# First transposes on two engines, a five-step key choice and an earlier-fed tail in a hard-max attention kernel

## The chip, the cores and the metric

The kernel runs on one core of a Trainium2 chip. The time is device microseconds (us) of one execution. An execution profile gives a span, about 1.8 us shorter than the time. A ratio is the mean time of one kernel's fast runs over the mean of the kernel before in the same rounds, with a 95% interval; it is therefore not quite the ratio of the medians that stand beside it.

The engines are PE (matmul), ACT (scalar engine), DVE (vector engine), POOL (it issues every gather here) and SP (it issues the stores). "PEclk" is the granted PE clock, as a share of full speed.

## The reference

```python
B, Sq, Sk, D = 4, 4096, 4096, 128        # q, k, v: float32
logits = np.matmul(q, k.transpose(0, 2, 1))
best = np.argmax(logits, axis=-1)        # one key for each query
return v[b_idx, best, :]                 # the value row of that key
```

## The kernel before

Queries are taken in 128 tiles of 128. For each tile, PE and ACT screen the keys in fp16, in groups of four keys; DVE folds the result into packed scores with the group's index in the low bits (`W`) and takes the eight best (`TOP`, a MAX8). For the best group the kernel then

1. computes the group's index on DVE (`cand`),
2. gathers that group's key differences with POOL (`kg`, one indirect gather per tile),
3. forms the dot products on DVE (`prod`, `p`, `p`, `D`, two tiles at a time: a "pair"),
4. picks the key within the group with a few small DVE operations, for a "piece" of eight or four tiles (`mx` ... `win`),
5. gathers the value rows with POOL (`vr`, one per tile) and stores them through SP.

Rows whose winner is uncertain are flagged and computed again in fp32. For the second half of the rows this happens at the very end: gathers `FR`, `FQ`, three `FK`, some DVE work, `FV`, then a branch on a count loaded from memory (`all_rows`, for rows too hard for this; not taken with these inputs), then one scatter of the repaired rows.

The parts that the change touches (`...` marks cuts):

```python
    for h in range(2):
        load_k(0, h, 0, 16)
    load_q(0, 0, 8)
    load_q(0, 8, NQT)
    ...
    def trn_half(b, u, h):            # transposes of k on PE; ACT alone copies them out
        ...
        if h == 1:
            nc.scalar.activation(out=kT[b % 2][:, u * 1024:(u + 1) * 1024], in_=ps, func=AF.Copy)

    def dots(c, x, m):
        ...
        yield "until", lambda: ("kg", x) in done, 2      # two tiles after the gather's place
        ...                                              # prod, p, p, D

    def pick(c, t0, t1):                                 # seven operations per piece
        ...
        nc.vector.tensor_reduce(out=mx[:, :, 0], in_=d, axis=AX_X, op=OP.max)
        nc.vector.scalar_tensor_tensor(out=near, in0=d, scalar=NEAR, in1=mx..., op0=OP.add, op1=OP.is_ge)
        nc.vector.tensor_reduce(out=CNT[:, t0:t1], in_=near, axis=AX_X, op=OP.add)
        nc.vector.tensor_tensor(out=lt, in0=d, in1=mx..., op=OP.is_lt)
        nc.vector.scalar_tensor_tensor(out=sel, in0=lt, scalar=float(1 << 20), in1=iotab[b]..., op0=OP.mult, op1=OP.add)
        nc.vector.tensor_reduce(out=wi, in_=sel, axis=AX_X, op=OP.min)
        nc.vector.scalar_tensor_tensor(out=win, in0=cand, scalar=4.0, in1=wi, op0=OP.mult, op1=OP.add)
        for j in range(n):
            late_q.append(lambda j=j: nc.gpsimd.indirect_dma_start(out=vr[:, j, :], out_offset=None, in_=v_flat,
                                                                   in_offset=IOA(ap=win[:, j:j + 1], axis=0)))
    ...
    def issue(it):                    # POOL's gathers of one tile: at most one key gather, then value gathers
        ...
        while near_q and (n < 1 or near_q[0] in marks):
            ...
        take_late(2 if n == 0 and len(late_q) > 4 or it >= T - 8 and it % 2 else 1)
    ...
    cuts = list(range(0, T - 16 + 1, 8)) + [T - x for x in (12, 8, 4, 0)]   # the pieces
    ...
    for it in range(T):               # the order of the instructions in one tile
        ...
        screen(it); fold(it - 1)
        step(it)                      # one operation of each running dots/pick
        top(it - 2)                   # MAX8
        gathers(it - 3)               # cand, and the key gathers into POOL's list
        step(it)
        issue(it)
    ...
    def flags_last(...):              # after the last MAX8
        ...
        late(LATE)                    # LATE = 8 value gathers first
        get(FR, rec, rr, P * T)
        get(FQ, q_flat, row, P * T)
        late(1)
        ...
        for r in range(3):
            get(FK[:, r, :], k4, gb[:, r:r + 1], B * NG)
        ...
        late(3)
        win = whole(exact(FK, FQ, gb, 3, "fe"))
        get(FV, v_flat, win, B * Sk)
        late(1 << 20)                 # all value gathers that are left
        ...
        all_rows()                    # the branch
        nc.gpsimd.indirect_dma_start(out=out_flat, out_offset=IOA(ap=rowk, axis=0), in_=FV, ...)
```

Of the kernel before, what the change touches and what calls it, by code (L numbers as in the profile page):

```python
# [7 lines left out]
FP32 = mybir.dt.float32  # L8
# [19 lines left out]
def kernel(ctx, tc, q, k, v, out):  # L28
# [6 lines left out]
    NG = Sk // 4  # L35

    k4 = k.rearrange("b (g f) d -> (b g) (f d)", f=4)
# [16 lines left out]
    k16 = [dr.tile([NG, 384], FP16, name=f"k16_{b}") for b in range(B)]  # L54
# [13 lines left out]
    def put_k(b, h):  # L68
        if b >= B:
            return  # L70
        src = natk[b % 2][:, h].rearrange("p (g f) d -> p g f d", f=4)
        nc.vector.tensor_tensor(out=kd[:, h], in0=src[:, :, 1:4, :], in1=src[:, :, 0:1, :].to_broadcast([P, 4, 3, P]),
                                op=OP.subtract)
        kb16 = k16[b].rearrange("(h p n) d -> p h (n d)", p=P, n=4)
        nc.sync.dma_start(out=kb16[:, h], in_=kd[:, h].rearrange("p g f d -> p (g f d)"))
# [9 lines left out]
    for h in range(2):  # L85
        load_k(0, h, 0, 16)
    load_q(0, 0, 8)
    load_q(0, 8, NQT)
# [3 lines left out]
    for i in range(2):  # L92
        ps = pp.tile([P, 1024], FP32, tag="u", name=f"warm_{i}")
        for j in range(8):
            nc.tensor.matmul(out=ps[:, (j % 2) * 512:(j % 2 + 1) * 512], lhsT=wz[:, 0:P], rhs=wz, start=True, stop=True)

    ident = cp.tile([P, P], FP32, tag="ident")
    masks.make_identity(nc, ident)
    identh = cp.tile([P, P], FP16, tag="identh")
# [3 lines left out]
    for h in range(2):  # L103
        put_k(0, h)
    D_t = [cp.tile([P, 8, 4], FP32, name=f"D{i}", tag=f"D{i}") for i in range(3)]
# [4 lines left out]
    for W in W_t:  # L110
        nc.gpsimd.iota(out=W.bitcast(U16)[:, 0::2].rearrange("p (h m r) -> p h m r", h=2, m=4),
                       pattern=[[-NG // 2, 2], [-1, 4], [-4, P]], base=NG - 1, channel_multiplier=0)

# [6 lines left out]
    iotab = [iota(f"iotab{b}", 4, b * Sk) for b in range(B)]  # L120
    iota4 = iotab[0]
# [4 lines left out]
    nc.vector.tensor_copy(out=iota_h, in_=iota_r)  # L126
# [17 lines left out]
    def trn_half(b, u, h):  # L144
        x = 2 * (u // 2)
        if h == 0:
            tk_t[u] = pp.tile([P, 1024], FP32, tag="u", name=f"tk_{b}_{u}")
        ps = tk_t[u]
        for m in range(4):
            o = ps[:, h * 512 + m * P:h * 512 + (m + 1) * P]  # L150
            nc.tensor.matmul(out=o, lhsT=natk[b % 2][:, h, 4 * m + x, :], rhs=identh, start=True, stop=False)
            nc.tensor.matmul(out=o, lhsT=natk[b % 2][:, h, 4 * m + x + 1, :],
                             rhs=identn if u % 2 else identh, start=False, stop=True)
        if h == 1:
            nc.scalar.activation(out=kT[b % 2][:, u * 1024:(u + 1) * 1024], in_=ps, func=AF.Copy)
# [17 lines left out]
    def trn_q(b, g):  # L173
        if b >= B:
            return
        ps = pp.tile([P, 1024], FP32, tag="u", name=f"tq_{b}_{g}")
        for i in range(8):
            nc.tensor.matmul(out=ps[:, i * P:(i + 1) * P], lhsT=natq[b % 2][:, g * 8 + i, :], rhs=identh,
                             start=True, stop=True)
        nc.scalar.activation(out=qT[b % 2][:, g * 1024:(g + 1) * 1024], in_=ps, func=AF.Copy)  # L180
# [54 lines left out]
    def gather(c, t0, n):  # L235
        c0, c1 = chunks[c]
        if t0 == c0:
            cand_t[c] = sp.tile([P, c1 - c0], U32, tag=f"cand{c1 - c0}", name=f"cand_{c}", bufs=3)
        x = cand_t[c][:, t0 - c0:t0 - c0 + n]
        nc.vector.tensor_scalar(out=x, in0=TOP.bitcast(U32)[:, t0:t0 + n, 0], scalar1=NG - 1, scalar2=NG - 1,  # L240
                                op0=OP.bitwise_and, op1=OP.bitwise_xor)
        kg = rp.tile([P, n, 3, P], FP16, tag=f"kg{n}", name=f"kg_{t0}", bufs=8)
        assert len(kg_t) < 8
        kg_t[t0] = kg
        for j in range(n):
            near_q.append(lambda j=j: nc.gpsimd.indirect_dma_start(  # L246
                out=kg[:, j].rearrange("p f d -> p (f d)"), out_offset=None, in_=k16[t0 // NQT],
                in_offset=IOA(ap=x[:, j:j + 1], axis=0)))
        mark = lambda: done.add(("kg", t0))
        marks.add(mark)  # L250
        near_q.append(mark)
        start(dots(c, t0, n), "dots", c)

    def dots(c, x, m):
        c0 = chunks[c][0]
        d = D_t[c % 3]
        b = x // NQT
        yield "until", lambda: ("kg", x) in done, 2
# [14 lines left out]
    def pick(c, t0, t1):  # L273
        n = t1 - t0
        b, qt = t0 // NQT, t0 % NQT
        d = D_t[c % 3][:, 0:n, :]
# [9 lines left out]
        nc.vector.tensor_reduce(out=CNT[:, t0:t1], in_=near, axis=AX_X, op=OP.add)  # L286
        done.add(("cnt", c))
        yield "cnt",
        lt = sp.tile([P, n, 4], FP32, tag=f"lt{n}", name=f"lt_{c}")
        nc.vector.tensor_tensor(out=lt, in0=d, in1=mx.to_broadcast([P, n, 4]), op=OP.is_lt)  # L290
        yield "dve",
        sel = sp.tile([P, n, 4], FP32, tag=f"sel{n}", name=f"sel_{c}")
        nc.vector.scalar_tensor_tensor(out=sel, in0=lt, scalar=float(1 << 20),
                                       in1=iotab[b].unsqueeze(1).to_broadcast([P, n, 4]), op0=OP.mult, op1=OP.add)
        yield "dve",
        wi = sp.tile([P, n], FP32, tag=f"wi{n}", name=f"wi_{c}")
        nc.vector.tensor_reduce(out=wi, in_=sel, axis=AX_X, op=OP.min)
        yield "dve",
        win = sp.tile([P, n], U32, tag=f"win{n}", name=f"win_{c}")
        nc.vector.scalar_tensor_tensor(out=win, in0=cand, scalar=4.0, in1=wi, op0=OP.mult, op1=OP.add)  # L300
        vr = rp.tile([P, n, P], FP32, tag=f"vr{n}", name=f"vr_{c}", bufs=3 if n == 8 else 4)
        for j in range(n):
            late_q.append(lambda j=j: nc.gpsimd.indirect_dma_start(out=vr[:, j, :], out_offset=None, in_=v_flat,  # L303
                                                                   in_offset=IOA(ap=win[:, j:j + 1], axis=0)))

        def store():
            nc.sync.dma_start(out=out[b].rearrange("(p t) d -> p t d", p=P)[:, qt:qt + n], in_=vr)
            done.add(("out", c))
# [9 lines left out]
    def flag_segment(t0, t1, ready, stored):  # L318
# [9 lines left out]
        nc.vector.scalar_tensor_tensor(out=F, in0=CNT[:, t0:t1], scalar=1.5, in1=F, op0=OP.is_gt, op1=OP.max)  # L328
# [90 lines left out]
        nc.vector.tensor_scalar(out=bo, in0=row, scalar1=Sq.bit_length() - 1, scalar2=NG.bit_length() - 1,  # L419
# [3 lines left out]
        nc.vector.tensor_scalar(out=gi, in0=FR[:, 0:3], scalar1=NG - 1, scalar2=NG - 1, op0=OP.bitwise_and, op1=OP.bitwise_xor)  # L423
# [4 lines left out]
        for r in range(3):  # L428
            get(FK[:, r, :], k4, gb[:, r:r + 1], B * NG)
# [18 lines left out]
    def flags_last(t0, t1, win_last, late):  # L448
        S = t1 - t0
        H, F = LF["H"], LF["F"]  # L450
        nc.vector.scalar_tensor_tensor(out=F, in0=CNT[:, t0:t1], scalar=1.5, in1=F, op0=OP.is_gt, op1=OP.max)
# [51 lines left out]
        nc.vector.tensor_scalar(out=bo, in0=row, scalar1=Sq.bit_length() - 1, scalar2=NG.bit_length() - 1,  # L503
# [6 lines left out]
        nc.vector.tensor_scalar(out=gi, in0=FR[:, 0:3], scalar1=NG - 1, scalar2=NG - 1, op0=OP.bitwise_and, op1=OP.bitwise_xor)  # L510
        gb = fp.tile([P, 3], U32, tag="gb", name="gb_e")
        nc.vector.tensor_tensor(out=gb, in0=gi, in1=bo.to_broadcast([P, 3]), op=OP.add)
        for r in range(3):
            get(FK[:, r, :], k4, gb[:, r:r + 1], B * NG)
# [19 lines left out]
    def exact(kk, qq, grp, R, name):  # L534
        d = fp.tile([P, R, 4], FP32, tag=f"xd{R}", name=f"xd_{name}")
        for r in range(R):
            for f in range(4):
# [5 lines left out]
        nc.vector.scalar_tensor_tensor(out=ix, in0=grp.unsqueeze(2).to_broadcast([P, R, 4]), scalar=4.0,  # L543
                                       in1=iota4.unsqueeze(1).to_broadcast([P, R, 4]), op0=OP.mult, op1=OP.add)
# [23 lines left out]
    def all_rows():  # L568
# [4 lines left out]
        with tc.If(left > 0):  # L573
            for b in range(B):
                with tc.For_i(0, NQT, 1) as t:
# [5 lines left out]
                    nc.vector.tensor_scalar(out=g8, in0=w8, scalar1=NG - 1, scalar2=(NG - 1) | (b * NG),  # L581
                                            op0=OP.bitwise_and, op1=OP.bitwise_xor)
                    kk = fp.tile([P, 8, 512], FP32, tag="ak", name=f"ak_{b}")
                    for r in range(8):
                        nc.gpsimd.indirect_dma_start(out=kk[:, r, :], out_offset=None, in_=k4,
# [5 lines left out]

    for u in (1, 3, 0, 2):
        trn_half(0, u, 0)
    trn_half(0, 1, 1)
    trn_q(0, 0)
    trn_half(0, 3, 1)
    trn_half(0, 0, 1)
    dpart(0, 0)
    trn_half(0, 2, 1)
    dpart(0, 1)  # L600
    cuts = list(range(0, T - 16 + 1, 8)) + [T - x for x in (12, 8, 4, 0)]
# [29 lines left out]
    def step(it):  # L631
        waiting = [s for s in live if s["kind"] == "dots" and ready(s, it)]
        quota = 2 if len(waiting) > 1 else 1
        for s in list(live):
# [3 lines left out]
            else:  # L638
                advance(s, it, False)
# [17 lines left out]
    def issue(it):  # L657
# [3 lines left out]
        while near_q and (n < 1 or near_q[0] in marks):  # L661
            g = near_q.pop(0)
            n += g not in marks
            g()
# [3 lines left out]
        take_late(2 if n == 0 and len(late_q) > 4 or it >= T - 8 and it % 2 else 1)  # L668
# [13 lines left out]

    units = []
# [3 lines left out]
    for it in range(T):  # L687
# [8 lines left out]
        if open_units:  # L696
# [3 lines left out]
            u[2](*u[3:])  # L700
        if it in (1, 2, 3):
# [5 lines left out]
        if it >= 1:  # L707
            fold(it - 1)
        if it % NQT in (9, 13):
# [4 lines left out]
        if it >= 3:  # L714
            gathers(it - 3)
        step(it)
# [11 lines left out]
    gathers(T - 3)  # L728
    flush()
# [64 lines left out]
```

## Time and profile before

| | us |
|---|---|
| time, median of the first 3 runs | 471.13 (470.97 to 471.29) |
| span of the profile | 469.4 |
| first `W` starts / last MAX8 ends | 19.82 / 418.61 |
| from the last MAX8 to the end | 50.8 |

I call the end of the last MAX8 **X**. It divides the run into a loop, in which DVE is the limit, and a tail, which is a serial chain.

The windows view of the kernel before; each row is a stretch, its length, and the busy time (and the number of instructions) of each engine in it.

```profile
core 0: us, PE busy (x) PEld busy (x) DVE busy (x) ACT busy (x) POOL busy (x), PEclk, DMA share, GB/s
...
15.00:39.00 24.00, 22.78 (x110) 9.91 (x108) 15.29 (x15) 24.00 (x29) 5.06 (x7) 1.00 0.57 105
39.00:393.00 354.00, 326.79 (x1557) 143.61 (x1555) 353.04 (x668) 332.09 (x387) 242.66 (x260) 1.00 0.49 103
...
418.60:452.00 33.40, 1.70 (x12) 1.36 (x12) 18.29 (x105) 0.00 (x0) 25.13 (x26) 0.50 0.39 106
```

ACT has no gap from 15 to 39 us, DVE has almost none from 39 to 393, and in the tail POOL's 26 gathers fill the time. The timeline of ACT before shows the start: one engine copies out every transpose, and the first screening copy `A` comes at 15.08 us. A line gives start, duration, engine, source line, operation, destination and source.

```profile
12.35 1.02 ACT L180 ACTIVATE qT<-tq 128x1024 f16<-128x1024 f32 x1 [1.68 <-PE tq L178]
13.27 1.93 ACT L155 ACTIVATE kT<-tk 128x1024 f16<-128x1024 f32 x2
15.08 1.04 ACT L198 ACTIVATE A<-pd 128x1024 f16<-128x1024 f32 x1
```

The timeline of DVE before, inside the loop. This is how a small operation is to be priced: not by its duration but by the distance from its start to that of the next.

```profile
213.81 0.16 DVE L280 TENSOR_REDUCE mx<-D 128x8 f32<-128x32 f32 x1
213.90 0.54 DVE L261 TENSOR_TENSOR prod<-kg,natq 128x768 f16<-128x768 f16 x1
214.37 1.21 DVE L228 MAX8 TOP<-W 128x8 f32<-128x1024 f32 x1
215.50 0.14 DVE L240 TENSOR_SCALAR cand<-TOP 128x2 uint32<-128x2 uint32 x1
```

`mx` lasts 0.16 us but the next operation, which doesn't need it, starts 0.09 us later. The Trainium skill, "Perfetto Trace Analysis", section "Optimizing Scalar/DVE Operations", says the same: a profiled duration is about twice the engine's busy time, because the write-acknowledgement half overlaps with the next instruction.

The timeline of POOL before, in the tail: value gathers 1.25 us apart, then the flag gathers, then four value gathers behind `FV`.

```profile
423.68 0.94 POOL L303 DMA_INDIRECT vr<-in_v_dram,win  x1 [0.30 <-issue]
424.93 0.94 POOL L303 DMA_INDIRECT vr<-in_v_dram,win  x1 [0.30 <-issue]
...
433.66 1.09 POOL L495 DMA_INDIRECT FR<-rec,rr_e  x1 [0.30 <-DVE row_e L492]
...
445.87 1.00 POOL L495 DMA_INDIRECT FV<-in_v_dram,xw_fe  x1 [0.76 <-DVE hi L570]
...
450.93 0.94 POOL L303 DMA_INDIRECT vr<-in_v_dram,win  x1 [0.30 <-issue]
458.48 1.01 POOL L531 DMA_INDIRECT out_dram<-FV,rowk_e  x1 [6.62 <-SPq L573]
```

### The profile page before, as it was taken

Reading aid. Unit: us, or ns where it says so; the run is one execution under the profiler, and the core shown is the slowest. Engines: PE = TensorE matmul, PEld = TensorE weight load, DVE = VectorE, ACT = ScalarE, POOL = GpSimd, SP = SyncE. Lnnn points to the kernel's source line nnn. Section 1 sums busy time; section 2 is a strip of 40 time slices with the busy share of each in tenths; the row PEclk is TensorE's granted clock in tenths of the full one; section 3 lists DMA queues with packets and bytes.
Section 4 is the critical chain, followed back from the end, with each engine's and each line's share of the span. In section 5 each row is a group of like instructions: output and inputs, shape, how many; then the busy total and the mean of one; then the engine's idle time right before and its main releaser. Section 6 shows DMA issues by size and latency. Waiting matters only on the chain. (4 is left out here: it accounts for less than half of the span.)

```text
span 469.4 us, 6266 instructions
## 1 busy us (share of the span) xinstructions
PE 381.8 (81%) x1840; PEld 169.8 (36%) x1840; DVE 417.2 (89%) x845; ACT 379.7 (81%) x438; POOL 305.8 (65%) x345
## 2 busy tenths in 40 slices
PE   7999999999999889999998889999999889920000
PEld 3544444444444334444443434343333333300000
DVE  4189999999999999999999999999999999998400
ACT  1999999999999899999998889999999879910000
POOL 9124445876667887766677876667777567777740
PEclk9899999999999999999999999999999999975555
DMA  7913489462224969642336864232433132324320
GB/s 135 231 31 81 79 129 124 91 137 69 86 74 99 193 110 161 117 113 59 101 92 146 119 123 94 69 98 64 120 90 110 51 100 57 113 66 122 104 79 5
DMA packets 40776, 47.42 MB, mean 101 GB/s; under 512 B 24200, under 2 KB 32395, under 8 KB 40736
## 3 DMA queue, kind: packets, MB, share of 16 engines
q0 software_dynamic: 18464, 30.97, 33.9%
q1 hardware_dynamic: 22272, 16.00, 13.2%
q8 instruction: 15, 0.25, 0.2%
q14 instruction: 25, 0.20, 0.2%
HBM read 39.59 MB, written 12.19 MB: 110 GB/s over the span
## 5 line engine op out<-in xcount | busy, mean ns | idle before, releaser
L198 ACT ACTIVATE A<-pd 128x1024 f16<-128x1024 f32 x256 | 258.8, 1042 | 17.2 <-PE pd L189 17.0
L246 POOL DMA_INDIRECT kg<-k,cand x128 | 126.2, 986 | 100.5 <-DVE p L265 25.2
L224 DVE SCALAR_TENSOR_TENSOR W<-psn,E 128x1024 int16<-128x1024 f32 x128 | 167.6, 1309 | 13.1 <-ACT E L211 11.9
L189 PE MATMUL pd<-kT,qT 128*128 128x512 f16 x512 | 152.3, 379 | 15.1 <-ACT A L198 14.4
L189 PE MATMUL psn<-kT,qT 128*128 128x512 f16 x512 | 151.8, 378 | 14.0 <-ACT A L198 9.0
L228 DVE MAX8 TOP<-W 128x8 f32<-128x1024 f32 x128 | 157.5, 1231 | 0.0
L189 PEld LDWEIGHTS <-qT 128*128 128x128 f16 x1024 | 98.5, 97 | 162.0 <-issue 74.7
L208 PE MATMUL psn<-A,identh 128*128 128x512 f16 x512 | 152.1, 378 | 0.0
L303 POOL DMA_INDIRECT vr<-in_v_dram,win x128 | 126.5, 988 | 39.0 <-issue 37.2
L211 ACT ACTIVATE E<-psn 128x1024 int16<-128x1024 f32 x128 | 132.3, 1034 | 5.5 <-PE psn L208 5.1
L208 PEld LDWEIGHTS <-identh 128*128 128x128 f16 x512 | 49.6, 97 | 60.8
L261 DVE TENSOR_TENSOR prod<-kg,natq 128x768 f16<-128x768 f16 x64 | 35.7, 559 | 1.1 <-DMA kg<-k,cand 1.1
L265 DVE TENSOR_TENSOR p<-prod 128x384 f16<-128x384 f16 x64 | 22.9, 361 | 0.0
L270 DVE TENSOR_REDUCE D<-p 128x6 f32<-128x192 f16 x64 | 22.2, 349 | 0.0
L167 ACT ACTIVATE kT<-uk 128x256 f16<-128x256 f32 x48 | 20.1, 418 | 0.9 <-PE uk L164 0.9
L268 DVE TENSOR_TENSOR p<-p 128x192 f16<-128x192 f16 x64 | 16.4, 259 | 0.0
L163 PE MATMUL uk<-identh,natk 128*128 128x128 f16 x96 | 15.8, 218 | 0.5 <-ACT A L198 0.5
L63 POOL DMA_DIRECT2D natk<-in_k_dram x26 | 15.6, 603 | 0.9 <-POOLq L778 0.8
L66 POOL DMA_DIRECT2D natq<-in_q_dram x26 | 15.7, 607 | 0.0
L461 PE MATMUL fp_e<-n_e,tri 128*128 128x1 f32 x2 | 0.6, 361 | 16.2 <-DVE n_e L459 16.2
L164 PEld LDWEIGHTS <-natk 128*128 128x128 f16 x96 | 9.3, 97 | 7.6 <-issue 5.1
L163 PEld LDWEIGHTS <-natk 128*128 128x128 f16 x96 | 9.3, 97 | 5.6
(148 smaller groups left out, 146.8 us busy)
## 6 DMA issues: line engine op xcount, KB each, us to landing
out_dram<-vr SPq DMA_DIRECT2D x14, 512.0 KB, 2.9
k<-kd SPq DMA_DIRECT2D x8, 384.0 KB, 2.6
natk<-in_k_dram POOLq DMA_DIRECT2D x24, 128.0 KB, 3.7
natq<-in_q_dram POOLq DMA_DIRECT2D x24, 128.0 KB, 3.1
kg<-k,cand POOLq DMA_INDIRECT x128, 2.7
vr<-in_v_dram,win POOLq DMA_INDIRECT x128, 3.3
natk<-in_k_dram POOLq DMA_DIRECT2D x2, 512.0 KB, 7.0
out_dram<-vr SPq DMA_DIRECT2D x4, 256.0 KB, 2.1
```

The costliest lines, as they stand in the source:

```text
L163: nc.tensor.matmul(out=o, lhsT=natk[b % 2][:, h, 4 * m + x, :], rhs=identh, start=True, stop=False)
L189: nc.tensor.matmul(out=ps[:, n * 512:(n + 1) * 512], lhsT=qT[b % 2][:, qt * P:(qt + 1) * P], rhs=kT[b % 2][:, u * 1024 + n * 512:u * 1024 ...
L198: nc.scalar.activation(out=A, in_=ps, func=AF.Abs)
L208: nc.tensor.matmul(out=ps[:, n * 512:(n + 1) * 512], lhsT=identh, rhs=A[:, n * 512:(n + 1) * 512], start=False, stop=True)
L211: nc.scalar.activation(out=E, in_=ps, func=AF.Relu, scale=QSCALE)
L224: nc.vector.scalar_tensor_tensor(out=W_t[t % NW].bitcast(I16)[:, 1::2], in0=ps, scalar=QSCALE, in1=E, op0=OP.mult, op1=OP.max)
L228: nc.vector.max(out=TOP[:, t, :], in_=W_t[t % NW].bitcast(FP32))
L246: near_q.append(lambda j=j: nc.gpsimd.indirect_dma_start(out=kg[:, j].rearrange("p f d -> p (f d)"), out_offset=None, in_=k16[t0 // NQT], ...
L261: nc.vector.tensor_tensor(out=prod, in0=kg, in1=natq[b % 2][:, x - b * NQT:x - b * NQT + m, :].unsqueeze(2).to_broadcast([P, m, 3, P]), op ...
L265: nc.vector.tensor_tensor(out=p1, in0=prod[:, :, :, 0:64], in1=prod[:, :, :, 64:128], op=OP.add)
L270: nc.vector.tensor_reduce(out=d[:, x - c0:x - c0 + m, 1:4], in_=p2, axis=AX_X, op=OP.add)
L303: late_q.append(lambda j=j: nc.gpsimd.indirect_dma_start(out=vr[:, j, :], out_offset=None, in_=v_flat, in_offset=IOA(ap=win[:, j:j + 1], a ...
```

## The change

Its intent has three parts.

- **Start.** Load the first queries sooner, transpose in half-size tiles, and share their copies between ACT and DVE, so that screening begins earlier.
- **Key choice.** Store group indices multiplied by four, and let one sum over weights 8 to 11 count the near keys and name the winner: five small operations instead of seven. A sum of several weights could name a row outside the table, so the value gathers now carry a bounds check.
- **Tail.** In the last tiles use pieces of four, compute `cand` and gather keys a tile sooner, let the dot products follow after one tile instead of two, run two pick operations per step, and issue more value gathers per tile, so that fewer are left behind X. The value rows are also stored four tiles at a time instead of eight.

The core of the diff (cut; `...` marks cuts):

```diff
-    for h in range(2):
-        load_k(0, h, 0, 16)
-    load_q(0, 0, 8)
-    load_q(0, 8, NQT)
+    load_k(0, 0, 0, 16)
+    load_q(0, 0, 4)
 ...
+    load_k(0, 1, 0, 8)
+    load_k(0, 1, 8, 16)
+    load_q(0, 4, 8)
+    load_q(0, 8, NQT)
 ...
+    trn_half(1, 0, ALL, by_act)
+    trn_half(3, 0, ALL, by_dve)
+    trn_half(0, 0, ALL, by_act)
+    trn_q(0, 4, by_dve)
+    trn_half(2, 0, ALL, by_act)
+    put_k(0, 0)
 ...
+    trn_half(1, 1, (2, 3), by_act)
+    trn_half(3, 1, (2, 3), by_dve)
+    trn_half(0, 1, (2, 3), by_dve)
+    trn_half(2, 1, (2, 3), by_dve)
 ...
-        yield "until", lambda: ("kg", x) in done, 2
+        yield "until", lambda: ("kg", x) in done, 1 if x >= TAIL else 2
 ...
+        nc.vector.tensor_tensor(out=sel, in0=near, in1=iota8.unsqueeze(1).to_broadcast([P, n, 4]), op=OP.mult)
+        yield "dve",
+        nc.vector.tensor_reduce(out=CNT[:, t0:t1], in_=sel, axis=AX_X, op=OP.add)
 ...                                                  (lt, the old sel, wi and the old win go)
+        nc.vector.scalar_tensor_tensor(out=win, in0=CNT[:, t0:t1], scalar=float(b * Sk - 8), in1=cand, op0=OP.add, op1=OP.add)
 ...
-                                                                   in_offset=IOA(ap=win[:, j:j + 1], axis=0)))
+                                                                   in_offset=IOA(ap=win[:, i + j:i + j + 1], axis=0),
+                                                                   bounds_check=B * Sk - 1, oob_is_err=False))
 ...
-    cuts = list(range(0, T - 16 + 1, 8)) + [T - x for x in (12, 8, 4, 0)]
+    cuts = list(range(0, T - 32 + 1, 8)) + list(range(T - 28, T + 1, 4))
 ...
+        quick = it >= TAIL
 ...
-                advance(s, it, False)             (for picks)
+                if advance(s, it, False) and quick and s["kind"] == "pick" and s in live:
+                    advance(s, it, False)
 ...
-        while near_q and (n < 1 or near_q[0] in marks):
+        while near_q and (n < 1 + (it >= T - 28 and len(near_q) > 2) or near_q[0] in marks):
 ...
-        take_late(2 if n == 0 and len(late_q) > 4 or it >= T - 8 and it % 2 else 1)
+        take_late(2 if n == 0 and len(late_q) > 4 or it >= T - 24 and it % 2 == 0 else 1)
 ...
+    TAIL = T - 24
 ...
-        if it >= 3:
+        if 3 <= it <= TAIL:
             gathers(it - 3)
+        if it >= TAIL:
+            gathers(it - 2)
         step(it)
         issue(it)
```

## The prediction

> **What bounds it now.** Three stages (windows, timeline and waits views of before: 471.13 us, span 469.4).
> - Start, 0 to 39 us. ACT's first copy A starts at 15.08. Before it, k's second half lands at 8.96, the first queries at 11.27, and ACT alone copies the kT and qT tiles, 0.91 us apart. From 15 to 39 ACT is busy 24.0 of 24.0 us, one tile per 2.71 us; DVE waits for it.
> - Loop, to 418.6 us. DVE is busy 353.0 of 354.0 us (39 to 393), ACT 332.
> - Tail, 418.6 (last MAX8) to 469.4. POOL issues 26 gathers back to back, 1.25 us apart (0.94 busy, 0.30 between): four of keys, 16 of values, six for flagged rows. The last store then leaves at about 453.9, the final scatter at 458.48 (6.6 us of wait for the sync queue), and 10.9 us follow.
>
> **What the change does.**
> 1. Start. Queries 0 to 3 load right behind k's first half, so k's second half should land at about 9.6, the queries earlier. Five of nine half-size copies go to DVE. PE finishes k by about 10.8; the first A comes at about 11.6, and no kT copy sits between the first As (0.9 us more). Gain 4.2 us, handed through because ACT's pace afterwards is unchanged.
> 2. Key choice. Two fewer DVE operations per piece. Interleaved, one costs about 0.095 us (starts 213.81 to 213.90), not its 0.19 us duration. In the loop 105 such operations become 90: -1.4 us. But in the last 24 tiles dependent ones follow each other (+0.1 us each, about 1.2), and one pair's dot products (1.14) move from tail into loop. Loop: about 1 us longer.
> 3. Tail. By the instruction order, POOL keeps after the last MAX8 (X) 2 key, 11 value and 6 flag gathers: 19, not 26. With bounds checks I take 1.30 us per value gather (the checked flag gathers' distance). Eight value gathers end at X+13.2, DVE's row numbers are ready at X+12.4, so flag gathers start at X+13.5 (before X+15.1). FV goes out at X+25.7 (before X+27.3). No value gather follows it (before four), so the last store leaves at X+25.5 and the scatter at X+30.1, not X+39.9. Gain 9.8 us, landing times as in this trace. The Trainium skill, "DMA: Bandwidth & Descriptors", section on the anatomy of one gpsimd DMA, gives about 2.0 us fixed cost; the trace agrees (key gather's issue over at 423.37, its user starts at 425.21).
>
> **Sum.** 471.1 - 4.2 + 1.0 - 9.8 = 458.1; I say 458.2 us, 8 in 10 within 454.5 to 462.5. Nearly all is on the critical path: the start shifts everything, the tail is serial. Faster by over 2% (under 461.7) 0.88; within 2% 0.11; slower 0.01.
>
> **What would show it.** First A at 11 to 12.5 us, first W at 15 to 16.5 (19.82 before); last MAX8 near 415.5; POOL waiting for DVE just before the last key gathers, then 19 gathers; the scatter about 4.5 us after FV; no DVE idle time in the loop; lt and wi gone.
>
> **What would make it wrong.** The small transpose of queries 4 to 7 (needed by about 22 us) or DMA crowding stalling ACT early; DVE's first copies held up by POOL's iotas; POOL, slower with bounds checks, falling behind in the last 24 tiles; ACT, with 6% slack, becoming the limit; the scatter waiting longer for FV's landing or the sync queue; the 10.9 us end growing.

## More of the kernel before

The groups of POOL's gathers before (count, then busy time in us and the mean of one in ns, then idle time before them):

```profile
L303 POOL DMA_INDIRECT vr<-in_v_dram,win x128 | 126.5, 988 | 39.0 <-issue 37.2 <-DVE val L340 0.3 <-DVE F_e L451 0.3
L246 POOL DMA_INDIRECT kg<-k,cand x128 | 126.2, 986 | 100.5 <-DVE p L265 25.2 <-issue 23.4 <-DVE cand L240 19.3
```

## The result, and the profile after

| | before | after | difference |
|---|---|---|---|
| time, median (4 runs each) | 471.05 (470.95 to 471.29) | 467.41 (466.09 to 467.57) | -3.64 |
| span of the profile | 469.4 | 465.5 | -3.9 |
| first `W` | 19.82 | 16.44 | -3.38 |
| first `W` to X (the loop) | 398.79 | 404.85 | +6.06 |
| X to the end (the tail) | 50.8 | 44.2 | -6.6 |

The ratio is 0.9916 (0.9897 to 0.9934): 0.8% faster, within 2%. The prediction had 458.2 us and a range of 454.5 to 462.5, and gave 0.88 to a gain of over 2%. It was wrong. The start and the tail gained, though less than predicted, and the loop gave 6 us back.

The timeline of ACT after, at the start. The first `A` comes at 12.64 us, 2.4 us earlier than before.

```profile
11.36 0.60 ACT L158 ACTIVATE kT<-tk 128x512 f16<-128x512 f32 x1 [1.76 <-PE tk L152]
12.64 2.85 ACT L202 ACTIVATE A<-pd 128x1024 f16<-128x1024 f32 x3 [0.68 <-PE pd L193]
```

It comes a microsecond later than predicted because PE was through with `k` at 12.0 us, where the prediction had about 10.8. The 16 small matmuls of the last quarter started only at 10.93, when it had landed; those of the third quarter had taken PE from 9.62 to 10.7. The timeline of PE after:

```profile
10.93 0.23 PE L151 MATMUL tk<-identh,natk 128*128 128x128 f16 x1 [0.24 <-DMA natk<-in_k_dram]
```

The windows view after, in stretches like those of before:

```profile
39.00:393.00 354.00, 324.72 (x1544) 142.62 (x1543) 349.56 (x656) 328.90 (x384) 258.22 (x267) 1.00 0.49 105
...
421.30:447.00 25.70, 1.70 (x12) 1.36 (x12) 15.40 (x85) 0.00 (x0) 18.43 (x18) 0.50 0.31 87
```

From 39 to 393 us DVE was busy 3.5 us less than before, and POOL 15.6 us more (258.22 against 242.66). The timeline of DVE after shows what DVE did instead: it waited. The bracket gives the idle time and what ended it.

```profile
191.41 0.15 DVE L297 SCALAR_TENSOR_TENSOR win<-CNT,cand 128x8 uint32<-128x8 f32 x1
192.62 0.56 DVE L265 TENSOR_TENSOR prod<-kg,natq 128x768 f16<-128x768 f16 x1 [1.06 <-DMA kg<-k,cand]
...
345.91 1.22 DVE L232 MAX8 TOP<-W 128x8 f32<-128x1024 f32 x1
347.16 0.21 DVE L244 TENSOR_SCALAR cand<-TOP 128x2 uint32<-128x2 uint32 x1
347.28 0.34 DVE L274 TENSOR_REDUCE D<-p 128x6 f32<-128x192 f16 x1
...
348.73 0.15 DVE L284 TENSOR_REDUCE mx<-D 128x4 f32<-128x16 f32 x1
348.91 0.17 DVE L287 SCALAR_TENSOR_TENSOR near<-D,mx 128x16 f32<-128x16 f32 x1
...
356.77 0.25 DVE L272 TENSOR_TENSOR p<-p 128x192 f16<-128x192 f16 x1
358.84 0.56 DVE L265 TENSOR_TENSOR prod<-kg,natq 128x768 f16<-128x768 f16 x1 [1.82 <-DMA kg<-k,cand]
```

Three things are to be read there.

- **Key gathers arrive late**, twice by more than 1 us: 1.06 us near 192 and 1.82 us near 358 us.
- **`cand` now stands right behind the MAX8 it reads.** From the start of the MAX8 to the next start is 1.25 us (345.91 to 347.16) where it had been 1.13 us. Since `cand` is computed in the same tile as its MAX8, this happens in each pair of the last tiles.
- **A dependent pair costs double.** `near` needs `mx` and starts 0.18 us behind it; before, an operation that doesn't need `mx` stood between and started after 0.09 us.

The timeline of POOL after shows why the gathers were late. The key gathers stand in one queue with one and a half value gathers per tile, where there had been one, and without a gap between them.

```profile
355.06 0.96 POOL L250 DMA_INDIRECT kg<-k,cand  x1 [0.30 <-issue]
356.32 1.00 POOL L304 DMA_INDIRECT vr<-in_v_dram,win  x1 [0.30 <-issue]
357.62 1.00 POOL L304 DMA_INDIRECT vr<-in_v_dram,win  x1 [0.30 <-issue]
```

The last key gather that the `prod` at 358.84 needs was issued at 355.06 and landed 3.8 us later (`--dma`, that issue alone); the page of the profile after puts a key gather's median from issue to landing at 2.8 us. So about 1 us of this wait is a slow landing, and the rest is POOL's queue. Between 324 and 378 us POOL ran 41 instructions, one every 1.32 us. The Trainium skill, "Perfetto Trace Analysis", section "What "DMA-bound" means", describes such a stretch: an issuing engine that is solid with DMA slices is generating descriptors, and that time isn't data movement. The trace agrees: the DMA engines were busy 0.35 of the same stretch.

The groups of POOL's gathers after. A value gather is dearer by 79 ns (988 to 1067 in the mean); it carries the bounds check. A key gather carries none and is nearly unchanged.

```profile
L304 POOL DMA_INDIRECT vr<-in_v_dram,win x128 | 136.6, 1067 | 39.0 <-issue 37.5 <-DMA kg<-k,cand 0.6 <-DVE p L272 0.3
L250 POOL DMA_INDIRECT kg<-k,cand x128 | 127.4, 995 | 85.1 <-issue 26.6 <-DVE p L269 23.5 <-DVE cand L244 17.9
```

The timeline of POOL after, in the tail:

```profile
435.22 0.99 POOL L498 DMA_INDIRECT FR<-rec,rr_e  x1 [0.30 <-DVE n_e L510]
...
447.55 1.00 POOL L498 DMA_INDIRECT FV<-in_v_dram,xw_fe  x1 [2.19 <-DVE hi L573]
454.42 1.03 POOL L534 DMA_INDIRECT out_dram<-FV,rowk_e  x1 [5.87 <-issue]
```

No value gather follows `FV`, as intended. But the scatter comes 6.87 us after `FV`, where I had predicted about 4.5.

To see where the loop's 6 us arose I compared when each tile's `W` starts, after minus before: -3.38 (tile 0), -3.7 (30), -4.5 (56), -3.5 (58, behind the wait of 1.06), -4.05 (98), -3.2 (108), +0.13 (110, behind the wait of 1.82), +1.9 (118), +2.56 (126). Nearly all of the loss lies in the last 30 tiles. There, from the `W` of tile 98 to X, DVE took 94.4 us before and 101.1 us after. Splitting that stretch by the distance from each start to the next: dot products +3.1 (one more pair in the stretch, estimated at 1.2 from the other pairs' distances, and the wait of 1.82), MAX8 +1.4, pick +2.0, `cand` +0.3.

### The profile page after: what moved, and what is told of

The parts are those of the page before. It is cut to its first block, busy times and chain, and to the rows that moved or that the text cites. A ratio compares the mean times of both kernels' runs of the same rounds, so it can differ in the third digit from the quotient of the medians.

```text
span 465.5 us, 6396 instructions
## 1 busy us (share of the span) xinstructions
PE 380.2 (82%) x1834; PEld 168.3 (36%) x1834; DVE 417.8 (90%) x825; ACT 376.8 (81%) x437; POOL 318.1 (68%) x345
## 4 chain that ended last, share of the span: by engine, by line
DVE 31%; issue 23%; ACT 13%; PE 13%; DMA 9%; POOL 7%; POOLq 0%; DVEq 0%; ACTq 0%
DVE W L228 14%; ACT A L202 10%; PE psn L193 5%; DVE TOP L232 5%; PE psn L212 4%; DMA kg<-k,cand 4%; ACT E L215 4%; DMA vr<-in_v_dram,win 3%; DVE prod L265 3%; PE pd L193 3%; POOL kg L250 3%; POOL vr L304 2%; DVE D L274 2%; DVE p L269 2%; DMA natk<-in_k_dram 2%
## 5 line engine op out<-in xcount | busy, mean ns | idle before, releaser
L304 POOL DMA_INDIRECT vr<-in_v_dram,win x128 | 136.6, 1067 | 39.0 <-issue 37.5
L232 DVE MAX8 TOP<-W 128x8 f32<-128x1024 f32 x128 | 155.8, 1217 | 0.0
```

The source lines that it names most:

```text
L232: nc.vector.max(out=TOP[:, t, :], in_=W_t[t % NW].bitcast(FP32))
```

## The experiments

My theory after reading the traces: POOL is filled up in the last tiles by the bounds checks, the extra value gathers and the earlier key gathers, and DVE waits for it. Rivals: the instruction order on DVE (`cand` behind its MAX8, dependent picks) costs the loop by itself; the smaller pieces cost it; the new start or the new pick carries less than thought. All outputs are right.

### Four runs on a chip that stalled every kernel

The first four kernels (edits below, where they ran again) met a chip on which the kernel before took 499.4 to 515.9 us, with single waits of up to 4.6 us on ACT and 3.9 us on PE, in the loop, for which the profile names no cause on the core; the profiles from the other chips that I looked through for it (f1, g3, h1, i2) have none. The ratios came out as 1.0027 (0.9881 to 1.0173), 1.005 (0.9922 to 1.0179), 1.0059 (0.9905 to 1.0213) and 1.0195 (1.0047 to 1.0343). The first three intervals contain 1. The four were run again on another chip (f1 to f4). Only the start of e1's trace, ahead of the stalls, can be used: its first `W` came at 16.43 us.

> The kernel before with the start of the change alone. My theory: the start is worth what the first W shows (16.44 against 19.82 us) and nothing takes it back later, so 3.4 us faster, about 467.7, last MAX8 near 415.2. Rival (the loop absorbs an earlier start, because POOL or the loads set its pace): less than 2 us faster, 469 or more.

> The kernel before with the five-step key choice alone, value gathers with bounds check included, pieces and tail as before. Theory: DVE saves about 15 x 2 x 0.095 = 2.8 us in the loop and about 0.6 in the tail's picks, but the check adds 0.05 to 0.07 us to each value gather, which costs about 1 us of waiting near tile 57 and about 0.8 us in the tail: 1 to 2 us faster, 469.0 to 470.1. Rival (the check costs nothing): 3 us faster or more, under 468.2.

> The changed kernel without the bounds check on the value gathers (no index is out of range with these inputs). Theory: the check slows POOL by 0.05 to 0.07 us per value gather; where POOL is the limit (tiles 42 to 58 with loads between, and from tile 104 on) key gathers then come late. Without it the 1.06 us wait at tile 57 vanishes, the 1.82 us wait near tile 109 shrinks by a half or more, and the tail shortens by about 0.6 us: 2 to 3 us faster than the changed kernel, about 465. Rival (the tail's schedule alone made the loop longer): under 1 us faster, waits unchanged.

> The changed kernel with the last tiles' group gathers started after the second step of the tile instead of right behind its MAX8. Theory: the index operation stood right behind the MAX8 that it reads and cost 12 x 0.13 = 1.5 us of DVE time; another operation in between hides it, so the loop is about 1.5 us shorter, unless the later key gathers lengthen the wait near tile 109. 466, 1 to 1.5 us faster than the changed kernel. Rival (that dependence costs nothing, the extra operations do): no change, 467.4.

### One part of the change alone

**f1: the new start in the kernel before** (the load order, the half-size transposes on two engines, `put_k(0, 1)` moved; nothing else).

> The same kernel as e1, whose chip stalled its engines in many places; repeated to get a time. My theory: the first W comes 3.4 us earlier (e1 showed that too) and nothing takes it back: about 467.7, 3.4 us faster. Rival (the loop absorbs an earlier start): less than 2 us faster.

Measured: 469.15 us against 471.21, ratio 0.9956 (0.9925 to 0.9988). The first `W` came 3.35 us earlier and X 3.54 us earlier. But the tail grew from 50.8 to 51.8 us: `FR` left at X+15.60, not X+15.05. POOL's backlog of gathers at X isn't shortened by an earlier X. So the start alone is worth about 2.1 us by the medians (0.6 to 3.5 by the interval; the profiled spans differ by 2.5), and not the predicted 4.2.

**f2: the new pick in the kernel before, with its bounds check** (old pieces, old tail).

The edit in short, not word for word:

```diff
-  CNT = sum(near); lt; sel; wi; win = 4*cand + wi         (seven operations)
+  sel = near * iota8; CNT = sum(sel); win = CNT + (b*Sk - 8) + cand   (five)
+  value gathers: bounds_check=B * Sk - 1, oob_is_err=False
```

> The same kernel as e2, repeated for a time. Theory: five steps save about 2.8 us of DVE in the loop and 0.6 in the tail, the bounds check takes about 1 us back near tile 57 and 0.8 in the tail: 1 to 2 us faster. Rival (the check costs nothing): 3 us or more.

Measured: 470.56 against 471.21, ratio 0.9984 (0.9961 to 1.0007). The interval contains 1, so no gain is shown, where I had expected 1 to 2 us. The loop shortened by 1.9 us, more than the 1.4 of the prediction, but the tail grew by 1.2: `FR` at X+17.37. Most of what the pick saves on DVE is spent on POOL: by the check (h1, next), and by the backlog that an earlier X doesn't shorten (f1, and h2 below without any check: `FR` at X+16.87).

**h1: the bounds check alone in the kernel before.**

```diff
-  in_offset=IOA(ap=win[:, j:j + 1], axis=0)
+  in_offset=IOA(ap=win[:, j:j + 1], axis=0), bounds_check=B * Sk - 1, oob_is_err=False
```

> The kernel before with nothing but the bounds check added to its value gathers. Theory: a value gather's distance to the next grows by 0.05 to 0.07 us; that costs where POOL's queue is the limit: up to 1 us near tile 57 and 16 x 0.055 = 0.9 us in the tail: 0.8 to 2 us slower, 472.0 to 473.2. Rival (the check is free, the 3.1 us of the changed kernel without it had another reason): within 0.3 us of before.

Measured: 472.88 against 471.42, ratio 1.0032 (1.0018 to 1.0047). The loop kept its length (398.87 us, before 398.79; X came at 418.06 because the first `W` came 0.6 us earlier in this profile); `FR` left at X+16.90 instead of X+15.05. The group of value gathers in its profile has the same mean as in the changed kernel:

```profile
L303 POOL DMA_INDIRECT vr<-in_v_dram,win x128 | 136.6, 1067 | 39.0 <-issue 35.7 <-DVE p L265 0.9 <-DVE TOP L228 0.6
```

**h2: start and pick together, without the check** (an order of weights that can't leave the table, described below; old pieces, old tail).

> Start and five-step choice, no bounds check (made safe by the weights), pieces and tail as before: the change without its tail part. Theory: first W at 16.5, last MAX8 near 412.5 (loop 396), but POOL's queue does not follow: tail 51 to 52 us, so 464.5 to 466, and the tail part, compared with the changed kernel without check (464.3), is worth 0 to 2 us, not 9.8. Rival (the tail part gains its 8 to 10 us when the check is gone): 471 or more here.

Measured: 466.96 against 471.42, ratio 0.9904 (0.9889 to 0.9918). That is slightly slower than I had expected, but the two parts without the check and without the whole tail part are already as fast as the full change (0.9916; the intervals overlap).

### One part of the change undone

**f3: the changed kernel without the bounds check.** With these inputs no index leaves the table (the highest was 16380 of 16384 rows), so the results are right; in general it would need the other weights.

```diff
-  in_offset=IOA(ap=win[:, i + j:i + j + 1], axis=0),
-  bounds_check=B * Sk - 1, oob_is_err=False))
+  in_offset=IOA(ap=win[:, i + j:i + j + 1], axis=0)))
```

> The same kernel as e3, repeated for a time. Theory: without the check the 1.06 us wait at tile 57 vanishes, the 1.82 us wait near tile 109 shrinks by half or more, the tail shortens by 0.6 us: 2 to 3 us faster than the changed kernel, about 465. Rival: under 1 us faster, waits unchanged.

Measured: 464.28 against 471.21, ratio 0.9842 (0.9821 to 0.9863), 3.1 us below the changed kernel by the medians. X came 2.45 us earlier (418.84) and the wait near 358 us was gone; the tail changed by 0.25 us only. In the tail `FR` did leave 0.8 us and `FV` 1.0 us sooner after X, but `FV` took 3.9 us to land instead of 3.1. The runs agree on when that happens: where the last store leaves 0.41 us or more ahead of `FV` (the changed kernel, f4, g1, g2), `FV` lands after 3.05 to 3.12 us; where it leaves later than that but within 0.9 us of `FV` (f3, i1, h3, g3, h4, i2), after 3.7 to 4.3 us. No run moves the store alone, so this cause isn't shown. The group of value gathers:

```profile
L304 POOL DMA_INDIRECT vr<-in_v_dram,win x128 | 127.8, 999 | 39.0 <-issue 38.4 <-DVE tp_e L481 0.3 <-DVE H_e L445 0.3
```

The same check costs 1.5 us in the kernel before and 3.1 us here (by the ratios 0.74%, 3.5 us). In the kernel before it delays the tail alone; here POOL has next to no slack in the last tiles, and the delay turns into DVE's wait.

**f4: `cand` later.** The dots and picks of the step now stand between a MAX8 and the `cand` that reads it.

```diff
+        step(it)
         if it >= TAIL:
             gathers(it - 2)
-        step(it)
         issue(it)
```

> The same kernel as e4, repeated for a time. Theory: the index operation no longer stands right behind the MAX8 it reads; the loop is about 1.5 us shorter unless the later key gathers lengthen the wait near tile 109: 466, 1 to 1.5 us faster than the changed kernel. Rival: no change, 467.4.

Measured: 467.21 against 471.21, ratio 0.9915 (0.9881 to 0.9948): no gain. Yet the delay behind the MAX8 did disappear. The timeline of DVE:

```profile
345.72 1.22 DVE L232 MAX8 TOP<-W 128x8 f32<-128x1024 f32 x1
346.86 0.33 DVE L274 TENSOR_REDUCE D<-p 128x6 f32<-128x192 f16 x1
...
358.85 0.56 DVE L265 TENSOR_TENSOR prod<-kg,natq 128x768 f16<-128x768 f16 x1 [2.29 <-DMA kg<-k,cand]
```

The MAX8 is followed after 1.14 us instead of 1.25, but the `prod` comes at 358.85 where it came at 358.84: the wait has grown from 1.82 to 2.29 us, and a second one, of 1.09 us, has appeared at 406.31. So DVE waits 3.4 us in all for key gathers between 280 us and X, where it had waited 1.8. In the stretch from tile 98 to X, MAX8's part fell by 1.4 us and that of dots and `W`, which contains the waits, rose by 1.7; the sum stayed at 101.1. This is what it looks like when another engine is the limit: time saved on the waiting engine becomes waiting.

**g2: no check and `cand` later, f3 and f4 together.**

> No bounds check and the group gathers after the second step, together. Alone the first gave 3.1 us and the second 0.2. Theory: the second alone gave nothing because POOL's queue set the pace, its DVE gain turned into waits for key gathers; with POOL relieved about 1 us of it should show: 463.0 to 463.8. Rival (the MAX8 dependence is free): 464.3 as without check alone.

Measured: 463.13 against 471.51, ratio 0.9816 (0.9799 to 0.9833). With POOL relieved, the order on DVE is worth something: X 0.9 us earlier than in f3 (417.94), the tail 0.5 us shorter.

**g1: the pieces of the kernel before** (eight tiles up to tile 112).

```diff
-    cuts = list(range(0, T - 32 + 1, 8)) + list(range(T - 28, T + 1, 4))
+    cuts = list(range(0, T - 16 + 1, 8)) + [T - x for x in (12, 8, 4, 0)]
```

> The changed kernel with pieces of eight tiles until 16 are left, as before; all else of the tail stays. By the instruction order the queue on POOL after the last MAX8 is the same (2 key, 11 value, 6 flag gathers). Theory: three picks of five operations leave the loop (about 1.4 us of DVE) but POOL's queue sets the pace there, so little of it shows: 0 to 1.5 us faster than the changed kernel (466.0 to 467.4). Rival (pieces of four are what makes the loop longer): 3 us faster or more.

Measured: 468.05 against 471.51, ratio 0.9919 (0.9903 to 0.9936), the changed kernel's 0.9916 within the interval. Its profiled run was its slowest (470.62), so I don't split its trace. The smaller pieces neither win nor lose measurably in sum; the 0 to 1.5 us that I had expected from undoing them didn't show.

**g4: fewer value gathers per tile** in the last 24 tiles.

```diff
-  take_late(2 if n == 0 and len(late_q) > 4 or it >= T - 24 and it % 2 == 0 else 1)
+  take_late(2 if n == 0 and len(late_q) > 4 or it >= T - 8 and it % 2 else 1)
```

> The changed kernel without the extra value gathers per tile (two per tile only in every other of the last 8, as before). By the instruction order 14 instead of 11 value gathers are left after the last MAX8, two of them behind FV. Theory (the extra value gathers stand in front of key gathers): the wait for key gathers near tile 109 shrinks below 0.5 us and the last MAX8 comes 1.5 to 3 us earlier, but the tail grows by 3 to 4 us: 467.5 to 469.5. Rival (the wait has another cause): last MAX8 unchanged at 421, time 470 or more.

Measured: 470.50 against 471.51, ratio 0.9975 (0.9951 to 1.0). The wait near 358 us was gone and X came 2.2 us earlier (419.07), as the theory has it. But the gathers that were put off stood in the tail, which grew by 5.1 us where I had expected 3 to 4, so the time lies above the expected 467.5 to 469.5. The extra value gathers are thus the part that pays: 5.1 us of tail for 2.2 us of loop.

**i1: dot products two tiles behind the gather again**, except in the last eight tiles.

```diff
-        yield "until", lambda: ("kg", x) in done, 1 if x >= TAIL else 2
+        yield "until", lambda: ("kg", x) in done, 1 if x >= T - 8 else 2
```

> The changed kernel with the dot products two tiles behind their gathers until the last 8 tiles, not the last 24. Theory: POOL lags by more than a tile near tile 109 (flag gathers, checked value gathers), and one tile of slack is too little: with two the 1.82 us wait there falls under 0.4 us and the last MAX8 comes 1 to 2.5 us sooner. One more value gather is left after it (12 by the instruction order), +1.3 us at most. 465.5 to 467. Rival (POOL's throughput, not the slack, sets the pace): the wait only moves to later tiles, last MAX8 unchanged, 467.4 or more.

Measured: 466.56 against 471.33, ratio 0.9897 (0.9882 to 0.9912). The waits near 192 and 358 us were gone and X came 2.3 us earlier (418.98). The timeline of DVE at the place where the changed kernel waits:

```profile
355.83 0.24 DVE L272 TENSOR_TENSOR p<-p 128x192 f16<-128x192 f16 x1
356.00 1.21 DVE L232 MAX8 TOP<-W 128x8 f32<-128x1024 f32 x1
```

Where `prod` had waited 1.82 us behind that `p`, the MAX8 now runs at once. The tail took back 1.4 us (45.6 instead of 44.2): one more value gather is left, the last store leaves 0.67 us behind `FV` instead of 0.57 ahead of it, and `FV` takes 4.3 us to land instead of 3.1. The wait near 192 us lies before the edit takes effect; h3 below, with the same loop, doesn't show it either, and I don't count it as an effect of any edit.

Three different edits (f3, g4, i1) each remove the wait near 358 us and bring X 2.2 to 2.5 us forward. So these are not three costs to be added. It is one condition, a key gather that lands too late for a reader one tile behind it, and either a shorter queue or a longer distance removes it.

### The end: branch and scatter

**h3: the scatter ahead of the branch.**

```diff
-        all_rows()
         nc.gpsimd.indirect_dma_start(out=out_flat, out_offset=IOA(ap=rowk, axis=0), in_=FV, ...)
+        all_rows()
```

> The changed kernel with the last scatter ahead of the branch for hard rows instead of behind it. Theory: FV itself lands 3.1 us after its issue and the branch[...] takes most of the rest of the 6.9 us; now the scatter comes 3.2 to 3.5 us after FV and the branch runs while the scatter lands: 2 to 3.5 us faster than the changed kernel, 464 to 465.4. Rival (the last store or FV's landing alone sets it): scatter still 6 us or more after FV, time 467 to 467.5.

Measured: 468.91 against 471.42, ratio 0.9943 (0.993 to 0.9956), so slower than the changed kernel by the medians (the two intervals overlap a little; h4 below repeats the swap on g3 and is clearly slower); I had expected it to be faster. The timeline of POOL:

```profile
446.25 0.99 POOL L498 DMA_INDIRECT FV<-in_v_dram,xw_fe  x1 [1.94 <-DVE rowk_e L532]
450.74 1.03 POOL L533 DMA_INDIRECT out_dram<-FV,rowk_e  x1 [3.50 <-SPq L576]
```

The scatter did leave 2.4 us sooner, 4.49 us after `FV` instead of 6.87. But from the scatter to the end it took 15.4 us instead of 11.1. What the branch does on POOL stands in the trace. This is the view of its source line in the changed kernel (`--source L576`): operation, count, shortest, median and longest in ns, first and last start in us.

```profile
L576 POOLq EVENT_SEMAPHORE  x4: 17/43/1501, 449.0 to 450.7; - x4
...
L576 POOLq COMPARE_BRANCH  x1: 53/53/53, 448.5 to 448.5; - x1
...
L576 POOLq INC_SWDGE_SEM  x1: 2410/2410/2410, 450.8 to 450.8; - x1
```

The jump itself is short: POOL's next instruction follows after 0.5 us (448.52 to 449.02). At the end of the branch POOL then waits on the semaphores of its gathers (the 1501 ns end with `FV`'s landing, at 450.65), and runs one `INC_SWDGE_SEM` of 2.41 us before it goes on to the scatter. That instruction took 2.37 to 2.43 us at this place in every run. Ahead of the scatter the wait for `FV` costs nothing extra, because the scatter needs `FV` too; the `INC_SWDGE_SEM` is the 2.4 us that h3 saved there. Behind the scatter both count: 1.74 us of waiting for the scatter's own landing and 2.43 us of `INC_SWDGE_SEM` make up nearly all of the 4.3 us by which the end grew.

The Trainium skill, "Runtime: NRT & Kernel Launch", section "Instruction fetch mechanics", offers another cause: a taken branch to a target outside the fetched pages has to fetch it by DMA first. On POOL the trace leaves at most 0.5 us for that. On SP 3.0 us pass between the branch and the next instruction (448.44 to 451.44), which would fit a fetch, but SP was through at 451.97, before POOL's `INC_SWDGE_SEM` ended at 453.22; so in the changed kernel it didn't hold the scatter.

### Versions meant to be better

**g3** combines: no check, made safe in general; `cand` later; the second pick operation of a step behind the others; seven instead of eight value gathers ahead of `FR`. The weights are 8 to 11 in the first half of the tiles, and -11 to -8 with a matching offset in the second half, so that a sum over several near keys leaves the table on neither side: batches 0 and 1 have rows above them, batches 2 and 3 have rows below. A row with several near keys is flagged and repaired anyway.

```diff
-LATE = 8
+LATE = 7
-  in1=iota8...                                  scalar=float(b * Sk - 8)
+  in1=(iota8 if t0 < T // 2 else iota11)...     scalar=float(b * Sk + (-8 if t0 < T // 2 else 11))
-  bounds_check=B * Sk - 1, oob_is_err=False     (value gathers)
-  F = max(CNT > 12.0, F)                        (flags of the second half)
+  F = max(CNT < -12.0, F)
```

> A version meant to beat both: no bounds check, made safe by weights that cannot lead out of range (8 to 11 upwards in the first half, -11 to -8 in the second); group gathers after the second step; the pick's second operation of a step put after the other operations, so that dependent ones do not follow each other; seven instead of eight value gathers ahead of the flag gathers. Theory (DVE and POOL alternate as limit): about 462, 5 us faster than the changed kernel. If POOL alone sets the pace, 463.5 or more.

Measured: 462.34 against 471.51, ratio 0.9809 (0.9788 to 0.9829). X at 416.89, tail 43.5.

**h4: g3 with the scatter ahead of the branch.**

> The version g3 (462.3) with the scatter ahead of the branch. Theory: 2 to 3.5 us less, 459 to 460.4. If the time at the end belongs to the landing and not the branch: 462.

Measured: 464.56 against 471.42, ratio 0.9859 (0.984 to 0.9879): 2.2 us worse than g3, the same miss as in h3.

**i2: g3 with i1's dots, the old pieces and eight value gathers ahead of `FR`.**

> g3 (462.3) with the same two tiles of slack, pieces of eight until 16 tiles are left, and eight value gathers ahead of the flag gathers. Theory: no wait for key gathers in the loop (2.8 us in g3), three picks fewer (about 1 us), one more value gather in the tail (+1.25): 460 to 461.5. If POOL's throughput sets the pace: 462.3 or more.

Measured: 462.32 against 471.33, ratio 0.9811 (0.9798 to 0.9825). X came 2.1 us earlier than in g3 (414.78), the earliest of the kernels that keep the tail part, and the tail was 2.1 us longer (45.6), where I had expected about 1.25 us; the 460 to 461.5 of the expectation was missed. The two tie, 1.9% below the kernel before and 1.1% below the changed kernel; whether they pass 2% is within their intervals.

## Why the prediction was wrong

By the ratios to the kernel before, the parts add up as follows (each step is a difference of two measured ratios, so it carries both intervals, 0.15 to 0.32% each):

| step | runs | share of the time before |
|---|---|---|
| start alone | f1 | -0.44% |
| pick without the check, on top | h2 minus f1 | -0.52% |
| tail part, on top | f3 minus h2 | -0.62% |
| bounds check, on top | changed kernel minus f3 | +0.74% |
| sum: the change | changed kernel | -0.84% |

Point by point, as the prediction put it:

1. **"Gain 4.2 us, handed through."** The direction was right, the size not. The first `A` came at 12.64, not "about 11.6", because PE finished k at 12.0 and not at 10.8, and the first `W` gained 3.4 us. In time the start alone gave 2.1, because POOL's backlog lengthens the tail by about 1 us when X comes earlier; "the start shifts everything" was wrong.
2. **"Loop: about 1 us longer."** This is the step that failed most: it was 6.1 us longer. The term for dependent picks (1.2) was mis-sized, +2.0 being measured for picks in the last 30 tiles. The other terms were missing: about 1.4 us for `cand` right behind its MAX8, 1.8 us of waiting for key gathers in the last tiles of the loop and 1.1 us near 192 us, where the prediction had "no DVE idle time in the loop". The condition itself stood in the last paragraph, "POOL, slower with bounds checks, falling behind in the last 24 tiles", but as a risk, not as a sum. That sum could have been made before: in the last 24 tiles POOL gets one key gather and 1.5 value gathers per tile, and the first half's flag gathers. At 1.25 and 1.30 us each the first two alone take 3.2 us (an estimate), and DVE's tile takes 94.4 / 30 = 3.1 us. POOL had no slack left there, so with the flag gathers it had to fall behind, and a distance of one tile doesn't cover that; with two tiles (i1) the wait was gone.
3. **"With bounds checks I take 1.30 us per value gather."** Right: 1.00 busy and 0.30 between. But I applied it to the tail alone. Removing the check (f3) shows that it took 2.45 us from the loop and, net, 0.25 us from the tail.
4. **"Gain 9.8 us" in the tail.** It was 6.6. POOL did issue 19 gathers behind X, with none behind `FV`, and `FR` left at X+13.9 (predicted X+13.5) and `FV` at X+26.3 (X+25.7). The failed term is the last one: the scatter came 6.9 us after `FV`, not 4.5. I had tied it to the last store, which left early as predicted (X+25.7); but the scatter then waited for POOL's own chain: 3.1 us until `FV` had landed, 2.4 us of `INC_SWDGE_SEM` at the end of the branch, and 1.4 us of small steps. h3 shows the 2.4 us by taking them away. "The scatter waiting longer for FV's landing" stood among the risks; the `INC_SWDGE_SEM` stood nowhere.
5. **"DVE's first copies", "the small transpose", "ACT becoming the limit".** None of these risks became visible: ACT was busy 26.36 of 26.40 us from 12.6 to 39, and from 39 to 393 its busy time stayed below DVE's (328.9 against 349.6 us of 354).

In span: -3.4 + 6.1 - 6.6 = -3.9 us, measured -3.9. Predicted: -4.2 + 1.0 - 9.8 = -13.0.

What stays open: what the `INC_SWDGE_SEM` does that takes 2.4 us; whether the last store is what slows `FV`'s landing; and how the 1.06 us wait near 192 us comes and goes between kernels with the same loop up to there.

## What to carry to other kernels

When a change moves work from a serial tail into a loop, add up the queue of the engine that takes it, per tile, against the loop's time per tile; an engine that looks 31% idle over the loop (POOL, busy 242.66 of 354 us before, where a busy record of 0.94 us moreover stands for a pitch of 1.25) can have no slack in the tiles that matter. If a reader must then follow its gather closely, leave it more distance. Price a small DVE operation by the distance to the next start, and keep an unrelated operation between a producer and its reader; but look for another engine's queue first, because time saved on an engine that waits comes back as waiting (f4). A safety option on an instruction that is issued once per tile has a price: here a different choice of weights made it unnecessary and leaving the check out was worth 3 us (f3).

## What the Trainium skill lacked or had wrong

- No page gives the price of a bounds check on an indirect gather; it belongs to "DMA: Bandwidth & Descriptors". Measured: POOL busy 0.94 to 1.00 us per gather of 128 rows, 988 to 1067 ns in the mean of the group; 1.5 us of the kernel before (h1), 3.1 us of the changed one (f3).
- The same page gives about 2.0 us fixed cost for a POOL-issued DMA (section "Anatomy of one DMA — SWDGE (gpsimd) path") but not the pitch of indirect gathers back to back: 1.25 us without the check and 1.30 with it, which left POOL no slack in the last tiles here. From issue to landing the profile after has a median of 2.8 us for key gathers; about 1 us of that is POOL's own busy time, so the page's figure roughly agrees.
- "VectorE: DVE Perf Modes", section "The DRAIN you can't avoid", measures eight copies with and without a semaphore after each and finds the same time. No page tells what a small operation costs that reads the result of the one just before it: here 0.18 us from start to start, against 0.09 us when it doesn't read it, and 0.1 us more for a `cand` right behind its MAX8.
- "Advanced Engine Details and Errata", section "Control Flow Timing", gives about 108 ns for a compare-and-branch. The record of POOL's in the changed kernel lasts 53 ns, and the next instruction follows after 0.5 us, so the jump isn't the cost of the branch.
- No page mentions `INC_SWDGE_SEM`, which POOL ran at the end of the branch, after waiting for all its gathers: 2.37 to 2.43 us in every run, 2.4 us of the way to the scatter.
